# A two-layer encoder on one core: both MLPs begin with two of seven products for eight slab pairs, with the results and the weight sums in DRAM

## The chip, the cores and the metric

The kernel runs on one NeuronCore of one Trainium2 chip. The time is device microseconds of one execution. It was 1729.74 us before, the median of three runs (1729.57 to 1729.74).

## The reference

A trunk of two encoder layers runs over two request groups with shared weights. Each group has 16 meta tokens in front, so there are 272 + 528 = 800 tokens of width 1024. The mixer of layer 0 is latent attention (16 heads); that of layer 1 is grouped-query attention in a window of 128, with sinks. A squared-ReLU MLP follows in both.

```python
def sqrelu_mlp(x, w1, w2):          # 1024 -> 4096 -> 1024
    h = jax.nn.relu(x @ w1)
    return (h * h) @ w2

for i in range(DEPTH):              # DEPTH = 2
    mix = mla_mixer(...) if i % 2 == 0 else gqa_mixer(...)
    h = layer_norm(DN_ALPHA * h + mix, ln1_g[i], ln1_b[i])
    h = layer_norm(DN_ALPHA * h + sqrelu_mlp(h, mlp_w1[i], mlp_w2[i]), ln2_g[i], ln2_b[i])
return h[:, N_META:]
```

All inputs and outputs are float32.

## The kernel before

**Numbers.** A product of float32 matrices is made of three matmuls (`mm3`, lines 547 to 549). Each operand is split into a rounded part and what is left: ScalarE casts the high part (line 1558 for weights, 1601 for activations) and VectorE subtracts (1564, 1603). The tiles `wsp` and `wspi` hold split weights, `h` and `h2` split activations, `w` and `wa` are banks of PSUM.

**Strassen's products.** The 800 tokens lie as columns in two halves of 400 (384 in layer 1, whose meta tokens are dropped). W1's 4096 columns are 32 slabs of 128. A pair of slabs with a pair of halves is a product of 2 x 2 blocks, done with seven products of blocks in place of eight (Winograd's form). It needs sums of weight blocks (`weight_add`, line 1575), sums of activations (`right_operands`, lines 1703 and 1691) and sums of results (`plus`, line 1785; `minus`, line 1609). `up_pair` does this for a pair; `down_group` does W2 likewise for two pairs at a time and adds into `acc` (lines 1869 and 1871). One pair's seven products have 12 matmuls each.

**The start of an MLP.** When an MLP begins, half 0 of the tokens is normed and half 1 is not. Its LayerNorm (`layer_norm`) is a chain: a matmul that gives the mean (line 1644), eight subtractions, squares, and sums of squares (1646, 1652, 1654), a matmul with ones (1661), root and reciprocal, a matmul that spreads the scale (1670), eight multiplications (1675). The sum over channels, `ssum` and `sqsum`, has been added up on GpSimd (line 1384) while the out-projection of the attention wrote `acc`. TensorE meanwhile has four slabs, `UP_FIRST`, done the plain way (eight products of eight): `up_slab` for half 0, and later for half 1, then `down_first` with four rows of W2. The other 28 slabs follow in six groups of two pairs and a last one (`LAST`).

```python
for j in UP_FIRST:
    F[j, 0] = split_hidden(up_slab(j, 0, ws[j], twos, fill.get(j)))
for k in range(4):
    right_operands(k)
for j in range(UPN):
    F[j, 1] = split_hidden(up_slab(j, 1, w, ...))
down_first()
for g, js in enumerate(GROUPS):
    down_group(g, [{} for _ in js], js)
```

**What sets the order.** `Plan` collects tasks with an engine, a cost, and what each reads and writes. It then writes out one order for every engine. TensorE's order comes from a table (`ORDERS`); the others' order, and for some sums the engine (`either`: VectorE or GpSimd), come from the planner's costs. Each engine works through its list in order, and so does the queue of SyncE (SP), which has all loads and stores of the MLPs. Weights pass through four raw tiles (`wraw`) and four split tiles; `sq` tiles hold results on the way.

Of the kernel before, what the change touches and what calls it, by code (L numbers as in the profile page):

```python
# [2756 lines left out]
```

## Time and profile before

| | |
|---|---|
| median of three runs | 1729.74 us |
| profiled execution | 1731.45 us, of which span 1729.7 us |
| granted TensorE clock | 0.998 |
| busy: TensorE, VectorE, ScalarE, GpSimd | 1715.9, 1427.1, 1022.0, 273.8 us |
| MLP 0, MLP 1 | about 449 to 917, 1231 to 1690 us |

A timeline row has the start, the busy time, engine, line, operation, what it writes and reads, shape and count, and in brackets the idle time of the engine before it and what ended that. In rows of groups the bar parts the names from busy time, mean ns of one, and idle time. In windows each engine has its busy time in the stretch, with the number of instructions; then come TensorE's granted clock, the busy share of the DMA engines and what they moved. A row of DMA issues has the KB of one transfer and the microseconds from issue to landing.

### The profile page before, as it was taken

To read this page: it belongs to the slowest core of one execution; us is meant where nothing else is said; L and a number is where in the kernel's file an instruction comes from. 1 tells how busy PE (TensorE), PEld (TensorE's weight loads), DVE (VectorE), ACT (ScalarE), POOL (GpSimd) and SP (SyncE) were. 2 spreads that over 40 slices of the span, in tenths; PEclk is the share of its full clock that TensorE was granted. 3 is DMA by queue.
4 is the path that set the end of the run, shared out by engine and by line. 5 is a ranking of instruction groups with operands and counts; after the bars stand their busy time and mean duration, and the time that the engine had idled before them with its cause. 6 is when DMAs were issued, how large, how long until landed. Compare 5 with 4: busy or idle time off the path is not lost.

```text
span 1729.7 us, 28705 instructions
## 1 busy us (share of the span) xinstructions
PE 1715.9 (99%) x10826; PEld 1619.1 (94%) x10826; DVE 1427.1 (83%) x2916; ACT 1022.0 (59%) x2176; POOL 273.8 (16%) x311
## 2 busy tenths in 40 slices
PE   9999999999999999999999999999999999999998
PEld 8999999989999999999999998889989889988996
DVE  7788878776878889899886978876887898899977
ACT  6577777773746446545644728775655446554652
POOL 1243222322200000000002233232200000000000
PEclk9999999999999999999999999999999999999999
DMA  6111100105211221222112321112211221221122
GB/s 232 59 41 32 32 26 26 40 30 170 95 57 54 74 74 62 74 74 74 62 67 99 102 90 53 38 38 83 101 55 56 74 72 64 73 86 61 62 81 90
DMA packets 39019, 122.32 MB, mean 71 GB/s; under 512 B 4704, under 2 KB 9952, under 8 KB 38752
## 3 DMA queue, kind: packets, MB, share of 16 engines
q1 hardware_dynamic: 38448, 120.09, 20.4%
q8 instruction: 85, 1.39, 0.3%
q14 instruction: 54, 0.44, 0.1%
q10 hardware_dynamic: 432, 0.39, 0.1%
HBM read 117.32 MB, written 3.15 MB: 70 GB/s over the span
## 4 chain that ended last, share of the span: by engine, by line
PE 96%; DVE 3%; ACT 1%; DMA 0%; issue 0%; SPq 0%; DVEq 0%; ACTq 0%
PE w L548 18%; PE w L547 18%; PE w L549 18%; PE wb L547 4%; PE wb L548 4%; PE wb L549 4%; PE wa L547 3%; PE wa L549 3%; PE wa L548 3%; PE wa L1291 2%; PE wa L1258 2%; PE sa L547 2%; PE sa L548 2%; PE sa L549 2%; PE wb L2459 2%; PE wb L2441 1%
## 5 line engine op out<-in xcount | busy, mean ns | idle before, releaser
L1871 DVE TENSOR_TENSOR acc<-acc,w 128x400 f32<-128x400 f32 (+1 forms) x306 | 184.8, 620 | 32.7 <-PE w L549 30.9
L548 PE MATMUL w<-h,wspi 128*128 128x400 f32 x320 | 110.3, 345 | 0.0
L547 PE MATMUL w<-h,wspi 128*128 128x400 f32 x320 | 110.1, 344 | 0.0
L549 PE MATMUL w<-h,wspi 128*128 128x400 f32 x320 | 110.1, 344 | 0.0
L548 PE MATMUL w<-h,wsp 128*128 128x400 f32 x312 | 107.7, 345 | 0.0
L547 PE MATMUL w<-h,wsp 128*128 128x400 f32 x312 | 107.6, 345 | 0.0
L549 PE MATMUL w<-h,wsp 128*128 128x400 f32 x312 | 107.4, 344 | 0.0
L1603 DVE TENSOR_TENSOR h<-sq,h 128x384 fp32r<-128x384 f32 (+1 forms) x163 | 91.2, 571 | 10.6 <-ACT h L1601 10.0
L1601 ACT CAST h<-sq 128x384 fp32r<-128x384 f32 (+1 forms) x163 | 82.8, 519 | 23.7 <-DVE sq L1609 13.8
L1200 ACT ACTIVATE p<-sa,nm,rq 106x528 f32<-106x528 f32 (+1 forms) x80 | 63.4, 794 | 24.4 <-DVE nm L1197 22.4
L547 PE MATMUL w<-wsp,h 128*128 128x512 f32 (+1 forms) x178 | 69.6, 391 | 0.8 <-DVE acc L1871 0.8
L549 PE MATMUL w<-wsp,h 128*128 128x512 f32 (+1 forms) x178 | 69.4, 390 | 0.0
L548 PE MATMUL w<-wsp,h 128*128 128x512 f32 (+1 forms) x178 | 69.4, 390 | 0.0
L547 PE MATMUL w<-wspi,h 128*128 128x512 f32 x174 | 69.0, 396 | 0.0
L549 PE MATMUL w<-wspi,h 128*128 128x512 f32 x174 | 68.8, 395 | 0.0
L548 PE MATMUL w<-wspi,h 128*128 128x512 f32 x174 | 68.8, 395 | 0.0
L1196 DVE TENSOR_REDUCE nm<-sa 106x1 f32<-106x528 f32 (+1 forms) x80 | 55.7, 701 | 14.8 <-PE sa L549 14.2
L547 PE MATMUL sa<-k,q 128*106 128x264 f32 (+5 forms) x208 | 62.7, 301 | 1.6 <-ACT p L1200 1.4
L1782 ACT COPY sq<-w 128x400 f32<-128x400 f32 (+1 forms) x71 | 34.5, 486 | 49.2 <-PE w L549 48.5
L1227 POOL TENSOR_TENSOR p<-p,rs 106x512 f32<-106x512 f32 (+1 forms) x40 | 42.0, 1049 | 129.6 <-DVE pk L1218 93.3
L547 PEld LDWEIGHTS w<-h,wspi 128*128 128x128 f32 x320 | 60.1, 188 | 0.0
L548 PEld LDWEIGHTS w<-h,wspi 128*128 128x128 f32 x320 | 60.1, 188 | 0.1
(847 smaller groups left out, 6086.8 us busy)
## 6 DMA issues: line engine op xcount, KB each, us to landing
wrawo<-in_w_o_dram SPq DMA_DIRECT2D x32, 512.0 KB, 3.3
wraw0d<-in_w2b_dram SPq DMA_DIRECT2D x24, 512.0 KB, 3.3
wraw1d<-in_w2b_dram SPq DMA_DIRECT2D x18, 512.0 KB, 3.3
wrawq<-in_w_q_dram SPq DMA_DIRECT2D x8, 512.0 KB, 3.3
xr<-in_xT_dram SPq DMA_DIRECT2D x16, 200.0 KB, 3.4
wraw<-in_w_qn_dram SPq DMA_DIRECT2D x8, 384.0 KB, 3.0
wx1d<-in_w2b_dram SPq DMA_DIRECT2D x6, 512.0 KB, 4.4
out_dram<-fo SPq DMA_DIRECT2D x11, 256.0 KB, 2.1
```

The costliest lines, as they stand in the source:

```text
L547: first = nc.tensor.matmul(out, lh, rh, start=start, stop=False, **kw)
L548: nc.tensor.matmul(out, lh, rl, start=False, stop=False, **kw)
L549: last = nc.tensor.matmul(out, ll, rh, start=False, stop=stop, **kw)
L1196: plan.task("DVE", DVE(528), lambda: V.tensor_reduce(nm.t[:qm, 0:1], v(), axis=AX.XY, op=ALU.max, negate=True), reads=[ps], writes=[nm], n ...
L1200: lambda: S.activation(P_().rearrange("p (a b) -> p a b", b=264), v(), AF.Exp, bias=nm.t[:qm, 0:1], scale=sc, accum_out=rs.t[:qm, 0:1]),
L1227: f = lambda row=row, r=r, w=w: G.tensor_tensor(row()[:, META:T], row()[:, META:T], r().to_broadcast([qm, w]), ALU.mult)
L1258: nc.tensor.transpose(ps.t[:, k * qm : (k + 1) * qm], src[k], ident[:qm, :qm])
L1291: nc.tensor.matmul(av[64 * e : 64 * e + 64, :n], vt.t[:, k, h0 + 64 * e : h0 + 64 * e + 64], PT.t[:, e, k, :n], start=k == 0, stop=False, ...
L1601: plan.task("ACT", 530, lambda: S.copy(d.t[:, 0], c.t[:, :n]), reads=[c], writes=[(d, "hi")], new=[d])
L1603: "DVE", 570, lambda: V.tensor_tensor(d.t[:, 1], c.t[:, :n], d.t.bitcast(F32)[:, 0], ALU.subtract),
L1871: f = lambda: V.tensor_tensor(z, z, ps.t[:, : z.shape[-1]], ALU.add)
L2459: nc.tensor.matmul(av[64 * gi : 64 * gi + 64, :256], at["V"][:, kbs[k][0], gc : gc + 64], PT.t[:, a : a + 256], start=k == 0, stop=False, ...
```

## The change

`UP_FIRST` becomes the eight even slabs from 0 to 14, which stand for eight pairs, and every pair goes by seven products. The signs of the Winograd form change, so that two of the seven products use only half 0 (`B1`), one with a plain block of W1 each. `head_pair` does these two for all eight pairs while half 1 is normed; the results leave through ScalarE (the second also through ReLU and square) and are stored to DRAM (`keep`, line 1808). In the groups `cross` does one more product, with a sum of weights that is loaded for two pairs at a time, and `rest_pair` does the other four; both fetch the kept results (`fetch`, line 1811). The three parts of the LayerNorm are put in after 1, 8 and 10 half products (`hooks`).

The eight pairs' weight sums, and those of W2 for two groups (`PRESUMS`), are made in DRAM: `presum` puts 24 transfers of 1 MB a layer into GpSimd's queue, each row of 2048 floats; 12 copy and 12 add to what is there. Layer 0's run during attention 0, layer 1's early in MLP 0. `halves` loads the sums as two blocks of 256 KB. The slab loop's `up_slab` and `down_first` go, and there are seven groups. For the pairs left, `weight_add` gives way to `sum_on`, in one instruction for 1024 columns where there were two of 512. The number of `sq` tiles goes from 6 to 8, all four tables of TensorE's order are new, and the planner has one more resource, `SUM`, with 10 us for a transfer.

```diff
-UP_FIRST = (3, 0, 1, 2)
-UPN = len(UP_FIRST)
+UP_FIRST = (tuple(range(0, 16, 2)), tuple(range(0, 16, 2)))
+SQ = (8, 8)
 LAST = 28
-GROUPS = [(j, j + 2) for j in range(UPN, LAST, 4)]
+PRESUMS = 2
+SUM_TIME = 10000
+GROUPS = [(j, j + 2) for j in range(0, LAST, 4)]
...
 ORDERS = [
-    "0 3 2 4-5 8 6 9 7 1 12-13 11 10 16 14 17 15 20 19 18 23 21-22 29 24 26-28 30 32 31 25 33 35 37-40 36 34 41 46 42 45 44 47-49 51 "
+    "0 3 2 4-5 8 6 9 7 1 12-13 11 10 16 14 17 15 20 19 18 23 21-22 29 24 26-28 30 32 31 25 33 35 37-38 34 36 39-41 46 42 45 44 47-49 51"
...
+    presums = [
+        {"up": spill.tile([4, len(UP_FIRST[l]), P, 512], F32, tag=f"us{l}", name=f"us{l}"), "down": spill.tile([4, PRESUMS, P, 1024], F32, tag=f"ds{l}", name=f"ds{l}")}
...
+    def presum(plan, l, last):
...
+                    op = {"accum_op": ALU.add} if key in seen else {}
...
+                    f = lambda x=x, a=a, op=op, out=out, c=c: nc.gpsimd.dma_start(out[x, c], a, **op, **size)
+                    plan.task("POOL", 1500, f, reads=[*reads, *last], writes=[on])
+                    plan.task("SUM", SUM_TIME, lambda: None, reads=[on], writes=[key, ("sum", l)])
+                    last = [("sum", l)]
...
-            split_weights(ua, lo, a, lo)
-            weight_add((a, lo), (a, lo), (b, lo), ALU.subtract, 512)
-            weight_add((b, lo), (b, lo), (b, hi), ALU.add, 512)
+            sum_on((a, lo), (b, lo))
+            sum_on((b, lo), (b, hi))
...
+        def keep(i, x, c):
+            plan.task("SP", 2600, lambda: nc.sync.dma_start(kept[i, x], c.t[:, :n]), reads=[c], writes=[("kept", i, x)])
+
+        def fetch(i, x, c):
+            plan.task("SP", 2600, lambda: nc.sync.dma_start(c.t[:, :n], kept[i, x]), reads=[("kept", i, x)], writes=[c], new=[c])
+            return c
...
+        def head_pair(i, w, ps):
...
+                    yield product(ps, w, lo, B1, 0, True, False, True, ks)
+                    if ks[-1] == 3:
+                        copy(a, ps)
+                        keep(i, 0, a)
...
+                    yield product(ps, w, hi, B1, 4, False, True, False, ks)
+                    if ks[-1] == 3:
+                        copy(c, ps, AF.Relu, 1.0)
+                        square_slow(c)
+                        keep(i, 1, c)
...
+        def rest_pair(i, D):
...
+            ua = halves(f"{j}x", summed(0, i), summed(1, i))
+            a, r = fetch(i, 0, tmp(f"a{l}_{j}r")), tmp(f"r{l}_{j}")
+            product(X, ua, lo, Ts[0], 0, True, False, True)
...
+            D[1] = split_hidden(fetch(i, 1, tmp(f"c{l}_{j}s")))
+            product(X, ua, hi, Ts[1], 0, False, False, False)
...
+            ub = halves(f"{j}y", summed(2, i), (w1[j + 1][:, hi], []))
+            product(X, ub, lo, Ts[2], 0, False, False, False)
...
+            c = fetch(i, 1, tmp(f"c{l}_{j}r"))
...
+            product(X, ub, hi, B2, 0, False, True, False)
...
+        hooks = {1: mean, 8: sums, 10: scale}
+        if l == 0:
+            presum(plan, 1, [(("h", 1, 7), "lo")])
```

**VectorE at the LayerNorm of MLP 0, before.** `acc` is the half being normed, `w_1` the mean's bank, `sq_0` and `sq_1` the two running sums of squares, `wspi` a split weight.

```order
L1646 TENSOR_TENSOR acc<-acc,w_1_5637 128x400 x4
L1564 TENSOR_TENSOR wspi_687<-wraw0f_5633,wspi_687 128x1024
L1646 TENSOR_TENSOR acc<-acc,w_1_5637 128x400 x2
L1652 TENSOR_TENSOR sq_1_5671<-sq_1_5671,sq_3_5682 128x400
L1646 TENSOR_TENSOR acc<-acc,w_1_5637 128x400 x2
L1652 TENSOR_TENSOR sq_0_5657<-sq_0_5657,sqsum_5240 128x400
L1652 TENSOR_TENSOR sq_0_5657<-sq_0_5657,sq_3_5682 128x400
L1652 TENSOR_TENSOR sq_1_5671<-sq_1_5671,sq_4_5697 128x400
L1654 TENSOR_TENSOR sq_0_5657<-sq_0_5657,sq_1_5671 128x400
L1564 TENSOR_TENSOR wspi_724<-wraw0f_5640,wspi_724 128x1024
L1665 RECIPROCAL rst_5623<-rst_5623 100x4
```

**The same, after.**

```order
L1674 TENSOR_TENSOR acc<-acc,w_1_5682 128x400 x6
L1680 TENSOR_TENSOR sq_1_5704<-sq_1_5704,sq_3_5718 128x400
L1674 TENSOR_TENSOR acc<-acc,w_1_5682 128x400 x2
L1680 TENSOR_TENSOR sq_0_5694<-sq_0_5694,sq_5_5725 128x400
L1680 TENSOR_TENSOR sq_0_5694<-sq_0_5694,sqsum_5253 128x400
L1680 TENSOR_TENSOR sq_1_5704<-sq_1_5704,sq_2_5707 128x400
L1682 TENSOR_TENSOR sq_0_5694<-sq_0_5694,sq_1_5704 128x400
L1589 TENSOR_TENSOR wspi_689<-wraw0f_5679,wspi_689 128x1024
L1589 TENSOR_TENSOR wspi_726<-wraw0f_5684,wspi_726 128x1024
L1693 RECIPROCAL rst_5653<-rst_5653 100x4
```

The split of a weight that stood between the subtractions now stands behind the chain's last sum.

**GpSimd at the end of attention 0, before.** `p` is a softmax tile, `ssum` and `sqsum` the sums over channels of the first and the second half.

```order
L1227 TENSOR_TENSOR p_4997<-p_4997,rs_4998 104x512
L1384 TENSOR_TENSOR ssum_4697<-acc 128x400
L1384 TENSOR_TENSOR ssum_4697<-ssum_4697,acc 128x400 x4
L911 TENSOR_TENSOR sqa_5323<-sqa_5323,sqa_5335 128x400
L911 TENSOR_TENSOR sqa_5332<-sqa_5332,sqa_5348 128x400
L1384 TENSOR_TENSOR sqsum_5240<-acc 128x400
L1384 TENSOR_TENSOR sqsum_5240<-sqsum_5240,acc 128x400 x4
L1703 TENSOR_TENSOR tsum_5635<-acc 128x400
L1652 TENSOR_TENSOR sq_0_5657<-sq_0_5657,sq_2_5674 128x400
```

**The same, after.** `ds` is the DRAM tile with the sums of W2, `in_w2q` the weights in the order in which they are added.

```order
L1251 TENSOR_TENSOR p_5009<-p_5009,rs_5010 104x512
L967 DMA ds_869<-in_w2q_dram 128x2048 x2
L1408 TENSOR_TENSOR ssum_4710<-acc 128x400
L1408 TENSOR_TENSOR ssum_4710<-ssum_4710,acc 128x400 x2
L967 DMA ds_869<-ds_869 128x2048
L1408 TENSOR_TENSOR ssum_4710<-ssum_4710,acc 128x400 x2
L967 DMA ds_869<-in_w2q_dram 128x2048
L911 TENSOR_TENSOR sqa_5350<-sqa_5350,sqa_5363 128x400
L911 TENSOR_TENSOR sqa_5360<-sqa_5360,sqa_5375 128x400
L1408 TENSOR_TENSOR sqsum_5253<-acc 128x400
L967 DMA ds_869<-ds_869 128x2048
L1408 TENSOR_TENSOR sqsum_5253<-sqsum_5253,acc 128x400
```

Transfers now stand between the additions to `ssum` and `sqsum`; one with `ds` on both sides reads what an earlier one made.

**SP's queue early in MLP 0, before.** All rows are loads of W1 and W2.

```order
L1533 DMA wraw0a_5769<-in_w2a_dram 128x1024
L1533 DMA wraw_4a<-in_w_0_dram 128x1024
L1533 DMA wraw_4b<-in_w_0_dram 128x1024
L1533 DMA wraw_6a<-in_w_0_dram 128x1024
L1533 DMA wraw_6b<-in_w_0_dram 128x1024
L1533 DMA wraw0d_6221<-in_w2b_dram 128x1024
```

**The same, after.** `us` is the DRAM tile with the sums of W1.

```order
L1558 DMA wraw0f_5729<-in_w_0_dram 128x1024
L1808 DMA kept_5654<-sq_6_5727 128x400
L1808 DMA kept_5656<-sq_3_5718 128x400
L1558 DMA wraw0f_5771<-in_w_0_dram 128x1024
L1558 DMA wraw0f_5791<-in_w_0_dram 128x1024
L1808 DMA kept_5658<-sq_5_5725 128x400
L1839 DMA wraw_x_5821<-us_868 128x512 x2
L1808 DMA kept_5655<-sq_4_5722 128x400
L1808 DMA kept_5660<-sqsum_5253 128x400
L1839 DMA wraw_0x<-us_868 128x512 x2
L1839 DMA wraw_2x<-us_868 128x512 x2
L1839 DMA wraw_0y<-us_868 128x512
```

Stores of kept results now stand between the loads of slabs and of weight halves.

More of the change, by code (lines that the diff above doesn't have):

```diff
@@ L148 @@
 class Plan:
-    LAG = {"PE": 198, "DVE": 45, "ACT": 45, "POOL": 50, "SP": 0}
+    LAG = {"PE": 198, "DVE": 45, "ACT": 45, "POOL": 50, "SP": 0, "SUM": 0}
     CHANGE = {
@@ L157 @@
     }
-    OVER = {"PE": 0, "DVE": 82, "ACT": 100, "POOL": 30, "SP": 0}
+    OVER = {"PE": 0, "DVE": 82, "ACT": 100, "POOL": 30, "SP": 0, "SUM": 0}
     last, count = {}, 0
@@ L477, in tile_encoder @@
     wp = pool("wp")
+    spill = pool("spill", space=bass.MemoryType.DRAM)
     banks = {}
@@ L1476, in attention0 @@
                     after0[o, i]()
-        ahead = [t.weights(ins["w1_0"][j], f"up{j}") for j in UP_FIRST[:2]]
+        ahead = [t.weights(ins["w1_0"][j], f"up{j}") for j in UP_FIRST[0][:2]]
         for x in ahead:
@@ L1482, in attention0 @@
             plan.issue(after)
-        for j, x in zip(UP_FIRST, ahead):
+        for j, x in zip(UP_FIRST[0], ahead):
             W.give(("up", j), x.t)
@@ L1569, in wparts, with sum_on @@
             return [h, *[(p, x) for p in parts(h, c) for x in ("hi", "lo")]]
[L1571 to L1576 removed]
+        def sum_on(out, x):
+            (r, c), key = out, parts(*out)
+            either(c.stop - c.start, lambda e: e.tensor_tensor(r.t[:, c], r.t[:, c], x[0].t[:, x[1]], ALU.add), reads=[*key, *parts(*x)], writes=key)
         lo, hi = slice(0, 512), slice(512, 1024)
@@ L1758, in residual, with up_tools, product @@
             return transposes
-        def up_pair(j, operands, beside=None, over=()):
-            ua, ub, uc, w22 = up_weights(j)
-            B = [([x[:, hf] for x in h], "h", hf) for hf in range(2)]
-            Ts = [([x[:, i] for x in T], "T", i) for i in range(3)]
-            def product(ps, w, c, X, k0, start, stop, fresh):
+        B1, B2 = [([x[:, hf] for x in h], "h", hf) for hf in range(2)]
+        Ts = [([x[:, i] for x in T], "T", i) for i in range(3)]
+        def up_tools(over=()):
+            def product(ps, w, c, X, k0, start, stop, fresh, ks=range(4)):
                 x = X[0]
                 def run():
-                    for k in range(4):
+                    for k in ks:
                         a = c.start + k * P
@@ L1776, in run @@
                         )
-                reads = [*wparts(w, c), *acts(X[1], X[2], range(k0, k0 + 4))]
-                plan.task("PE", 12 * MM, run, reads=reads, writes=[ps], new=[ps] if fresh else [], ends=over)
-            def copy(d, ps, f=AF.Copy):
-                plan.task("ACT", 500, (lambda: S.copy(d.t[:, :n], ps.t[:, :n])) if f is AF.Copy else (lambda: S.activation(d.t[:, :n], ps.t[:, :n], f)), reads=[ps], writes=[d], new=[d])
+                reads = [*wparts(w, c), *acts(X[1], X[2], [k0 + k for k in ks])]
@@ L1784, in plus, with copy @@
+                plan.task("PE", 3 * len(ks) * MM, run, reads=reads, writes=[ps], new=[ps] if fresh and ks[0] == 0 else [], ends=over)
+            def copy(d, ps, f=AF.Copy, scale=-1.0):
+                plan.task(
+                    "ACT", 500, (lambda: S.copy(d.t[:, :n], ps.t[:, :n])) if f is AF.Copy else (lambda: S.activation(d.t[:, :n], ps.t[:, :n], f, scale=scale)),
+                    reads=[ps], writes=[d], new=[d],
+                )
             def plus(d, ps):
                 plan.task("DVE", 570, lambda: V.tensor_tensor(d.t[:, :n], d.t[:, :n], ps.t[:, :n], ALU.add), reads=[ps, d], writes=[d])
-            def square(d, relu=True):
-                if d in (a, r, b, e):
-                    if relu:
-                        plan.task("ACT", 510, lambda: S.activation(d.t[:, :n], d.t[:, :n], AF.Relu), reads=[d], writes=[d])
-                    plan.task("ACT", 510, lambda: S.activation(d.t[:, :n], d.t[:, :n], AF.Square), reads=[d], writes=[d])
-                    return
-                plan.task(
-                    "DVE", 575, lambda: V.scalar_tensor_tensor(d.t[:, :n], d.t[:, :n], 0.0, d.t[:, :n], ALU.max, ALU.mult),
-                    reads=[d], writes=[d], port=True,
-                )
@@ new lines, in square @@
+            def square(d, scale=1.0):
+                if scale:
+                    plan.task("ACT", 510, lambda: S.activation(d.t[:, :n], d.t[:, :n], AF.Relu, scale=scale), reads=[d], writes=[d])
+                square_slow(d)
+            return product, copy, plus, square
+        def keep(i, x, c):
[3 more added lines that the diff above has]
+            return c
@@ new lines, in head_pair, with first, second @@
+        def head_pair(i, w, ps):
+            product, copy, plus, square = up_tools()
+            a, c = tmp(f"a{l}_{i}"), tmp(f"c{l}_{i}")
+            def first():
+                for ks in (range(0, 2), range(2, 4)):
+                    yield product(ps, w, lo, B1, 0, True, False, True, ks)
+                    if ks[-1] == 3:
+                        copy(a, ps)
+                        keep(i, 0, a)
+            def second():
+                for ks in (range(0, 2), range(2, 4)):
+                    yield product(ps, w, hi, B1, 4, False, True, False, ks)
[3 more added lines that the diff above has]
+                        keep(i, 1, c)
+            return first, second
@@ new lines, in halves, with summed @@
+        def halves(nm, *srcs):
+            r, w = new("wraw", lambda: wp.tile([P, 1024], F32, tag="wraw", name=f"wraw{l}_{nm}", bufs=WRAW)), weights(f"{l}_{nm}")
+            for x, (c, (src, key)) in enumerate(zip((lo, hi), srcs)):
+                plan.task("SP", 1900, lambda r=r, c=c, src=src: nc.sync.dma_start(r.t[:, c], src), reads=key, writes=parts(r, c), new=[r] if x == 0 else [])
+            for c in (lo, hi):
+                split_weights(w, c, r, c)
+            return w
+        def summed(x, i):
+            return presums[l]["up"][x, i], []
@@ L1798, in up_pair @@
+        def up_pair(j, operands, beside=None, over=()):
+            ua, ub, uc, w22 = up_weights(j)
+            product, copy, plus, square = up_tools(over)
             X, Y, Z = bank(f"ux{l}_{j}"), bank(f"uy{l}_{j}"), bank(f"uz{l}_{j}")
@@ L1807, in up_pair @@
                     tiles[j + o] = [None, None]
-            product(X, ua, lo, B[1], 0, True, False, True)
-            copy(a, X)
+                product(Z, uc, hi, B1, 4, True, True, True)
+                plus(a, Z)
+                square(a)
+                plain(0, 0, a)
+                product(X, ub, lo, Ts[1], 0, False, False, False)
+                copy(b, X)
+                product(X, uc, lo, Ts[2], 0, False, False, False)
+                copy(e, X)
+                product(X, w22, lo, B2, 0, False, True, False)
+                copy(r, X, AF.Relu)
+                square(r, False)
+                plain(1, 0, r)
+                product(Y, ua, hi, Ts[0], 0, True, False, True)
+                plus(e, Y)
+                square(e, -1.0)
+                plain(1, 1, e)
+                if beside is not None:
+                    beside()
+                product(Y, ub, hi, B2, 4, False, True, False)
+                plus(b, Y)
+                square(b)
+                plain(0, 1, b)
+                return
             product(Y, ua, hi, Ts[0], 0, True, False, True)
@@ L1856, in down_weights @@
-            weight_add((A11, c), (A21, c), (A11, c), ALU.add, w)
-            split_weights(out[5], c, A11, c)
-            A12 = raw(src[3, :, :w], f"{l}d{g}3", "wx" if l else "wraw")
-            weight_add((A21, c), (A12, c), (A21, c), ALU.subtract, w)
-            split_weights(out[3], c, A21, c)
-            split_weights(out[4], c, A22, c)
-            split_weights(out[2], c, A12, c)
+            get = lambda x, tag="wraw": raw(src[x, :, :w], f"{l}d{g}{x}", tag)
+            if g < PRESUMS:
+                out = {}
+                for x in DOWN_ORDERS[l]:
+                    i = {1: 0, 4: 2, 2: 3}.get(x)
+                    r = raw(presums[l]["down"][{5: 0, 7: 1, 6: 2, 3: 3}[x], g], f"{l}d{g}s{x}") if i is None else get(i)
+                    out[x] = weights(f"{l}d{g}_{x}")
+                    split_weights(out[x], c, r, c)
+                return out
@@ L1863, in down_weights, with accumulate @@
+            split_weights(out[3], c, A11, c)
+            for x in DOWN_ORDERS[l][5:]:
+                split_weights(out[x], c, A22 if x == 4 else A12, c)
             return out
         seen = set()
-        def accumulate(z, ps, place):
+        def accumulate(z, ps, place, op=ALU.add):
             if l == 0 and place not in seen:
-                f = lambda: V.scalar_tensor_tensor(z, z, ALPHA, ps.t[:, : z.shape[-1]], ALU.mult, ALU.add)
+                f = lambda: V.scalar_tensor_tensor(z, z, ALPHA, ps.t[:, : z.shape[-1]], ALU.mult, op)
@@ L1987, in mlp_middle @@
-        mean, sums, scale = layer_norm()
-        twos = [range(k, k + 2) for k in range(0, 8, 2)]
-        fill = {UP_FIRST[0]: {0: mean}, UP_FIRST[1]: {3: sums}, UP_FIRST[2]: {1: scale}}
-        F = {}
-        for j in UP_FIRST:
-            if j not in ws:
-                ws[j] = up_weight(j)
-            F[j, 0] = split_hidden(up_slab(j, 0, ws[j], twos, fill.get(j)))
+        mean, sums, scale = layer_norm()
+        kept = {(i, x): spill.tile([P, n], F32, tag=f"kept{l}{i}{x}", name=f"kept{l}{i}{x}") for i in range(len(UP_FIRST[l])) for x in range(2)}
@@ new lines, in mlp_middle @@
+        late = {}
+        hooks = {1: mean, 8: sums, 10: scale}
+        if l == 0:
+            presum(plan, 1, [(("h", 1, 7), "lo")])
+        made_ = 0
+        for p in range(0, len(UP_FIRST[l]), 2):
+            two = []
+            for i in (p, p + 1):
+                w = ws[UP_FIRST[l][i]] if UP_FIRST[l][i] in ws else up_weight(UP_FIRST[l][i])
+                two.append(head_pair(i, w, bank(f"ux{l}h{i}")))
+            for x in range(2):
+                for f in two:
+                    for _ in f[x]():
+                        made_ += 1
+                        if made_ in hooks:
+                            hooks[made_]()
@@ L1995, in mlp_middle, with crosses @@
+        turn = residual() if l else None
+        def crosses(i):
+            w = halves(f"x{i}", summed(3, i), summed(3, i + 1))
+            cross(i, w)
+            cross(i + 1, w)
+        crosses(0)
         for k in range(4):
             right_operands(k)
-        turn = residual() if l else None
-        for j in range(UPN):
-            w = up_weight(j) if j == UP_FIRST[0] else ws[j]
-            F[j, 1] = split_hidden(up_slab(j, 1, w, [range(k, k + 1) for k in range(8)] if j == 0 else [range(8)]))
@@ L2001, in mlp_middle @@
-        down_first()
-        for g, js in enumerate(GROUPS):
+        for g, js in enumerate(GROUPS):
+            if g == 0 and turn:
+                for hf, q in TURNS:
+                    turn(hf, q)
+            if js[0] in UP_FIRST[l] and js[0] // 2 not in late:
+                crosses(js[0] // 2)
             down_group(g, [{} for _ in js], js)
@@ L2603, in attention1 @@
                     after1[o, i]()
-        ahead = [weights(ins["w1_1"][j], f"up{j}") for j in UP_FIRST[:2]]
+        ahead = [weights(ins["w1_1"][j], f"up{j}") for j in UP_FIRST[1][:2]]
         for w in ahead:
@@ L2609, in attention1 @@
             plan.issue(after)
-        for j, w in zip(UP_FIRST, ahead):
+        for j, w in zip(UP_FIRST[0], ahead):
             W.give(("up", j), w.t)
```

270 lines of the change are left out of this document (127 added, 143 removed), and 73 rows, old and new, of the table ORDERS.

## The prediction

> **What bounds the kernel now.** I read the engines' busy shares first, then the chain that ended last, then windows by stage, and inside the stages single rows.
>
> ```profile
> span 1729.7 us, 28705 instructions
> PE 1715.9 (99%) x10826; PEld 1619.1 (94%) x10826; DVE 1427.1 (83%) x2916; ACT 1022.0 (59%) x2176; POOL 273.8 (16%) x311
> PE 96%; DVE 3%; ACT 1%; DMA 0%; issue 0%; SPq 0%; DVEq 0%; ACTq 0%
> ...
> core 0: us, PE busy (x) PEld busy (x) DVE busy (x) ACT busy (x) POOL busy (x), PEclk, DMA share, GB/s
> 380.00:449.10 69.10, 69.10 (x417) 66.78 (x416) 48.79 (x69) 32.96 (x55) 19.45 (x13) 1.00 0.43 141
> 449.10:480.00 30.90, 30.73 (x174) 29.88 (x173) 27.07 (x48) 24.61 (x48) 4.40 (x4) 1.00 0.16 55
> 500.00:900.00 400.00, 400.00 (x2196) 399.70 (x2195) 345.23 (x580) 205.42 (x359) 10.95 (x9) 1.00 0.19 66
> 1225.00:1260.00 35.00, 34.10 (x199) 32.27 (x198) 30.05 (x49) 24.91 (x54) 8.24 (x7) 1.00 0.29 95
> 1490.00:1540.00 50.00, 49.24 (x244) 43.73 (x243) 46.32 (x69) 26.87 (x48) 5.59 (x4) 1.00 0.20 64
> ```
>
> TensorE is idle for 13.8 us of 1729.7 and 96% of the chain is its own matmuls. In 500 to 900, inside MLP 0, it is never idle, at full clock. So a matmul less is worth its issue interval, as long as nothing else comes to hold TensorE. The next engine is VectorE: 345.23 of 400 us (86%). Where VectorE is fullest in MLP 1 (46.32 of 50 us, 93%), TensorE loses 0.76 us: that row is my measure of what a crowded VectorE costs. The second weak place is the LayerNorm ahead of each MLP, where everything behind the norm waits for a short serial chain.
>
> **Matmuls removed.** Products 1 and 2 of the eight pairs need only the half that is already normed, so they take the place of the plain slabs as cover, and four slabs a layer go from eight products in eight to seven. Counted in the two instruction orders, TensorE issues 48 matmuls of 400 columns, 24 of 384 and 18 of 512 fewer. The listed means overlap in the pipeline; the price is the distance between starts.
>
> ```profile
> 1250.82 0.34 PE L547 MATMUL w<-hc,wspi 128*128 128x384 f32 x1
> ...
> 1252.90 0.34 PE L547 MATMUL w<-hc,wspi 128*128 128x384 f32 x1
> ...
> 1344.90 0.40 PE L547 MATMUL w<-wsp,h 128*128 128x512 f32 x1
> ...
> 1347.00 0.40 PE L547 MATMUL w<-wsp,h 128*128 128x512 f32 x1
> ```
>
> 400 columns: 400.00/2196 = 0.182 us. 384: 12 starts in 2.08 us, 0.173. 512: 9 starts in 2.10 us, 0.233. So 48 x 0.182 + 24 x 0.173 + 18 x 0.233 = 8.7 + 4.2 + 4.2 = **17.1 us** off the path.
>
> **The LayerNorm's cover.** The norm's chain on VectorE, in both layers:
>
> ```profile
> 450.58 0.94 PE L1644 MATMUL w<-sqsum,part 128*128 128x400 f32 x2 [0.17 <-DVE sqsum L1384]
> ...
> 453.67 1.23 DVE L1564 TENSOR_TENSOR wspi<-wraw0f,wspi 128x1024 fp32r<-128x1024 f32 x1
> ...
> 459.18 0.58 DVE L1654 TENSOR_TENSOR sq<-sq,sq 128x400 f32<-128x400 f32 x1
> ...
> 460.08 0.79 PE L1661 MATMUL w<-ones,sq 128*100 128x1 f32 x8
> ...
> 1230.75 0.94 PE L1644 MATMUL w<-sqsum,part 128*128 128x400 f32 x2 [0.23 <-DVE sqsum L2499]
> 1239.99 0.87 PE L1661 MATMUL w<-ones,sq 128*100 128x1 f32 x8
> ```
>
> Before, 48 matmuls stand between the mean and the sums, which is 8.8 us, and the chain needs 459.76 - 450.58 = 9.2 us with a weight split of 1.23 us in its midst: they fit (0.17 us idle in 449 to 480). Now 36 stand there in layer 0 (6.6 us) and 42 in layer 1 (7.3 us), and the split has left the middle of the chain, which then needs about 9.2 - 1.2 = 8.0 us. With 0.4 us of the mean's own second piece the cover is 7.0 and 7.7, so TensorE would wait about 1.0 us in layer 0 and 0.3 in layer 1. Between the sums and the scale 12 matmuls stand instead of 6, so that wait can't grow. I take +1.3 us; bounds 0 (VectorE's other work in the chain goes too) and 2.2 + 1.5 = 3.7 (the chain stays at 9.2).
>
> **VectorE.** By the orders it issues 130 adds of 512 columns fewer, 52 operations of 1024 more, 47 more of 400 and 22 more of 384 columns.
>
> ```profile
> L1575 DVE TENSOR_TENSOR wraw0d<-wraw0d,wraw0d 128x512 f32<-128x512 f32 x46 | 30.9, 686 | 0.5 <-DMA wraw0d<-in_w2b_dram 0.5
> ...
> L1564 DVE TENSOR_TENSOR wspi<-wraw0d,wspi 128x1024 fp32r<-128x1024 f32 x21 | 25.6, 1221 | 1.6 <-ACT wspi L1558 1.6
> ...
> L1603 DVE TENSOR_TENSOR h<-sq,h 128x384 fp32r<-128x384 f32 x83 | 46.1, 572 | 3.8 <-ACT h L1601 3.6
> L1603 DVE TENSOR_TENSOR h<-sq,h 128x400 fp32r<-128x400 f32 x80 | 45.1, 571 | 6.8 <-ACT h L1601 6.4
> ```
>
> -130 x 0.686 + 52 x 1.221 + 69 x 0.571 = -89.2 + 63.5 + 39.4 = +13.7 us of work, in some 17 us less time. Over the 800 us that VectorE works in the two MLPs that is 814 in about 910, 89%: between the 86% that cost TensorE nothing and the 93% that cost 0.76 us in 50 (1.5%). The four groups a layer of kept pairs take 8 x 288 x 0.182 = 420 us; at 1.5% that is 6.4 us, at the 86% row nothing. I take +1.5, nearer the 86% row, because in the crowded stretch VectorE was also slowed by sums on GpSimd, and ends 0 and 6.4. ScalarE gains 48 operations and loses 40, and is 51% busy in 500 to 900: nothing, covered by matmuls.
>
> **DRAM sums.** 24 transfers a layer of 1 MB, from DRAM to DRAM, 12 copies and 12 that add. GpSimd issues them and waits in its queue for the one that a sum adds to. They lie beside other work; the price is zero if each lands in time. The nearest landings are loads and the final stores:
>
> ```profile
> wrawo<-in_w_o_dram SPq DMA_DIRECT2D x32, 512.0 KB, 3.3
> ...
> out_dram<-fo SPq DMA_DIRECT2D x11, 256.0 KB, 2.1
> ...
> wraw<-in_w_in_dram SPq DMA_DIRECT2D x3, 512.0 KB, 5.9
> ```
>
> From 2.1 and 3.3 us the slope is 1.2 us per 256 KB, so 1 MB takes 0.9 + 4.8 = 5.7 us and an adding one, with two reads, 0.9 + 9.6 = 10.5; in proportion to 512 KB, 6.6 and 13.2. The last row is the start of the kernel, where all loads are under way at once; in proportion to it an adding one would take 23.6. All are estimates: no row shows a DRAM-to-DRAM sum, and the middle ones are nearest: in 380 to 449 the engines are 0.43 busy at 141 GB/s, and the last eight sums, 4 x 1 + 4 x 2 = 12 MB in the 78 us up to 432, add 154 GB/s, by that row 0.47: nearly full, not over. The place that can't bear lateness is the end of attention 0. There the last sums stand between GpSimd's softmax multiplies and the additions whose result the mean waits for:
>
> ```profile
> 364.95 1.04 POOL L1227 TENSOR_TENSOR p<-p,rs 106x512 f32<-106x512 f32 x1 [3.69 <-DVE pk L1218]
> ...
> 407.36 2.17 POOL L1384 TENSOR_TENSOR ssum<-ssum,acc 128x400 f32<-128x400 f32 x2 [11.70 <-DVE acc L1377]
> ...
> 422.06 1.98 POOL L1384 TENSOR_TENSOR sqsum<-acc 128x400 f32<-128x400 f32 x1 [2.04 <-DVE acc L1377]
> 430.53 1.05 POOL L1384 TENSOR_TENSOR sqsum<-sqsum,acc 128x400 f32<-128x400 f32 x1 [6.50 <-DVE acc L1377]
> 436.91 3.26 POOL L1384 TENSOR_TENSOR sqsum<-sqsum,acc 128x400 f32<-128x400 f32 x2 [5.32 <-DVE acc L1377]
> 444.58 1.25 POOL L1384 TENSOR_TENSOR sqsum<-sqsum,acc 128x400 f32<-128x400 f32 x1 [4.42 <-DVE acc L1377]
> ```
>
> In the new order the 18th sum follows the multiply at about 365, and 20, 21, 22, 23 and 24 each wait for the one before, so the last issues no earlier than 366 + 5T (365 and its multiply), T being one transfer. It has its place at about 432: T may be 13.2 us for nothing. Behind it stand three additions, some 5 us, due shortly before the mean's matmul at 450.6, 449.9 with VectorE's last addition. With T from 5.7 to 13.2 I cost it at 0.
>
> **Loads and kept results.** SP issues 170 transfers more, 96 of them the kept results (32 stores, 64 fetches); most of the others are weight halves. A store stands in SP's queue until its result is squared, and the loads behind it wait. The DMA share is 0.19 in MLP 0 at 66 GB/s; layer 1's sums, which run there, move 12 x 1 + 12 x 2 = 36 MB, 77 GB/s over its 468 us, which by that row is 0.22 more: far from full. I cost this at nothing: cover is one weight product, 12 x 0.182 = 2.2 us, against a fetch of about 2 us issued a group earlier. If the cover is gone, a pair loses about 1 us (rival A).
>
> **The sum**, against the profiled execution (1731.45 us, 1.7 over the median of the runs): 1731.45 - 17.1 + 1.3 + 1.5 = 1717.15, and as a median 1717.15 - 1.7 = **1715.4 us**.
>
> **Rivals.**
>
> A. *The gain is eaten by VectorE and late loads.* A kept pair's five products take 60 matmuls, 10.9 us, for five weight halves, their splits and four kept results; before, 84 matmuls covered a pair's weights. For it: 1490 to 1540 above. Against it: 500 to 900, with no idle at 86%. Price: 6.4 us for VectorE and up to 1 us for each of 16 pairs, 22.4 in full. Half of it or all, added to the 1711 that the saving gives without any cost (below): 1722 to 1733.
>
> B, the other side. *The DRAM sums are slow and hold GpSimd's queue ahead of the LayerNorm's sum.* The mean matmul stands in TensorE's queue, so all stops. At T = 16 the last sum issues at 446, and about 1 us is lost; the gain is gone where 366 + 5T + 5 = 449.9 + 14.3, at T = 18.6 us; at the 23.6 us of the start's loads the loss is 39 us, which gives 1715 + 39 = 1754. Against it: the loads of 3.3 us. For it: the DMA engines then are nearly full, each adding transfer waits for the one before to have landed, so delays add five times, and the upper end lies beyond the point that decides. The Trainium skill, DMA: Bandwidth & Descriptors (Two DMAs through the same engine are not ordered), has the dependent transfer wait for the earlier one's semaphore, and its section Anatomy of one DMA says that this can come after a surprisingly long delay when the target is DRAM, although its figure for a transfer from GpSimd's queue (2.0 us plus bytes over 436e3) gives an estimate of 4.4 us for 1 MB. By the figure the sum stays at 1715.4, by the warning it would be B's 1754; no run of before has such a transfer.
>
> C. *The kept results change nothing*, because the LayerNorm's wait grows by what the matmuls save: it would need 7 to 8 us at each norm, three times the worst case above (2.2). About 1727 to 1731.
>
> **How the numbers follow.** Forecast (1709 to 1722) 0.69, A 0.15, B 0.12, C 0.04. Bounds of the forecast: all costs at zero and the 1.7 us idle in the two MLP 1 windows regained gives 1711, with 2 us left for what the trace can't resolve; upwards all ends in full, 3.7 and 6.4 us instead of 2.8, give 1723, where A begins. The range of 8 in 10 reaches into A: 1709 to 1729. A difference of 0.2%, 3.5 us, is about what can be told from no change: below 1726.3 lie the forecast and half of A, 0.77; within, 0.10, the other half of A with C; above 1733.2, 0.13, B and a remnant of A.
>
> **What would show it.** Right: some 90 matmul records fewer; TensorE without gaps in 500 to 880; sums landing in under 13 us; the mean's row 0.2 us after its sum; VectorE near 89% in the MLPs. Wrong: an idle time of several us ahead of the mean matmul put down to GpSimd's sum (B), gaps at first products of kept pairs put down to weight splits or fetches (A), over 2 us before the matmul with ones in either layer (C).

## The result, and the profile after

The changed kernel takes 1741.88 us (median of four runs, 1740.68 to 1743.99) against 1729.74: a ratio of 1.0069, interval 1.0051 to 1.0086. It is slower by 12 us, where 14 us less were forecast, and it lies outside the range of 1709 to 1729. The profiled execution took 1743.99 us.

The page of the profile after, its first lines, the DMA queues and the first rows of the DMA issues (KB of one, and us to landing):

```profile
span 1742.2 us, 29013 instructions
...
PE 1708.4 (98%) x10736; PEld 1609.0 (92%) x10736; DVE 1431.2 (82%) x2911; ACT 1027.0 (59%) x2184; POOL 299.2 (17%) x353
...
q1 hardware_dynamic: 62928, 157.20, 27.0%
q0 software_dynamic: 6912, 50.33, 11.2%
...
PE 89%; DVE 5%; DMA 4%; ACT 2%; issue 1%; SPq 0%; DVEq 0%; ACTq 0%
...
us<-in_w1q_dram POOLq DMA_DIRECT2D x24, 1024.0 KB, 8.7
...
ds<-in_w2q_dram POOLq DMA_DIRECT2D x12, 1024.0 KB, 8.2
```

TensorE's records are 90 fewer, as the orders say. But it is idle for 33.8 us instead of 13.8, and the chain that ended last now holds 4% of DMA, where before it held none. The times of the mean's matmul in the two layers divide the loss:

```profile
450.74 0.94 PE L1672 MATMUL w<-sqsum,part 128*128 128x400 f32 x2 [0.17 <-DVE sqsum L1408]
...
1254.54 0.94 PE L1672 MATMUL w<-sqsum,part 128*128 128x400 f32 x2 [0.23 <-DVE sqsum L2580]
```

Up to MLP 0 nothing has changed (450.58 before). From one mean to the other it is 803.8 us instead of 780.2: 23.6 more. From the second mean to the end it is 487.7 instead of 498.9: 11.3 less. So the same form of MLP wins in layer 1 and loses in layer 0. Windows over MLP 0, over a stretch in it, over MLP 1, and the end of attention 0 (columns as before: us, busy time of the engines, clock, DMA share, GB/s):

```profile
545.00:580.00 35.00, 22.47 (x91) 20.85 (x92) 15.82 (x28) 7.40 (x15) 2.75 (x4) 0.77 1.01 295
449.10:917.00 467.90, 447.42 (x2397) 441.69 (x2396) 393.60 (x653) 240.41 (x426) 25.57 (x32) 0.97 0.51 155
1231.00:1690.00 459.00, 458.60 (x2356) 416.90 (x2355) 409.91 (x639) 264.31 (x482) 36.54 (x31) 1.00 0.35 114
...
380.00:449.10 69.10, 69.10 (x418) 66.58 (x417) 48.00 (x73) 33.26 (x55) 20.00 (x19) 1.00 0.82 238
```

In MLP 0 TensorE is idle for 20.5 us; in 545 to 580 it does 91 matmuls in 35 us, and the DMA engines have no free time at all. What it waits for in MLP 0, the chain through that stretch, and GpSimd's timeline:

```profile
PE w L547 <- ACT sq L1793: 11.2, 5, 6.9
PE w L547 <- ACT wspi L1583: 7.1, 2, 5.1
...
461.08 16.19 DMA wraw0f<-in_w_dram
...
551.66 22.79 DMA wraw_6y<-in_w_dram
```

```profile
456.52 2.45 POOL L967 DMA_DIRECT2D us<-in_w1q_dram  x4
534.22 1.05 POOL L1636 TENSOR_TENSOR sq<-sq,sq 128x400 f32<-128x400 f32 x1 [75.25 <-DVE h L1626]
535.22 2.51 POOL L967 DMA_DIRECT2D us<-in_w1q_dram  x3
536.82 1.44 POOL L967 DMA_DIRECT2D us<-us  x1
544.27 0.55 POOL L967 DMA_DIRECT2D us<-us  x1 [6.01 <-DMA us<-in_w1q_dram]
```

The waits name ScalarE's splits and copies, but ScalarE was waiting itself: a load of 512 KB issued at 461.1 landed after 16.2 us, one of 256 KB issued at 551.7 after 22.8, where before loads of 512 KB took 3.3. Ahead of each, GpSimd had put four of layer 1's sums into its queue within some 3 us (at 456.5, and at 535.2 with a fifth at 544.3). In attention 0, softmax multiplies or other work stood between nearly all sums; in MLP 0, from 456 to 580, GpSimd's own work between them is one square. Layer 1's sums are not over early in MLP 0, either: the last are issued at 778. In 449 to 600 the sums themselves land after some 12 and 13 us, half as long again as on the whole:

```profile
us<-in_w1q_dram POOLq DMA_DIRECT2D x9, 1024.0 KB, 11.9
us<-us POOLq DMA_DIRECT2D x4, 1024.0 KB, 13.4
```

The stops cost more than themselves. TensorE's timeline behind two of them:

```profile
560.75 0.70 PE L547 MATMUL w<-t,wspi 128*128 128x400 f32 x1 [5.13 <-ACT wspi L1583]
...
575.54 0.70 PE L547 MATMUL w<-t,wspi 128*128 128x400 f32 x1 [6.89 <-ACT sq L1793]
576.04 0.54 PE L548 MATMUL w<-t,wspi 128*128 128x400 f32 x1
...
580.38 0.54 PE L549 MATMUL w<-t,wspi 128*128 128x400 f32 x1
580.71 0.44 PE L547 MATMUL w<-t,wspi 128*128 128x400 f32 x1
```

For 5.2 us after the second stop matmuls start 0.334 us apart instead of 0.182. Windows over four such stretches, behind stops of 2.0, 5.1, 6.9 and 2.0 us, have a granted clock of 0.50 to 0.62:

```profile
474.20:478.70 4.50, 3.83 (x12) 3.48 (x13) 2.95 (x5) 2.39 (x4) 0.00 (x0) 0.62 1.01 357
560.70:567.40 6.70, 6.41 (x18) 5.83 (x19) 4.88 (x10) 1.14 (x3) 0.82 (x1) 0.51 0.99 272
575.50:580.90 5.40, 5.36 (x16) 5.32 (x17) 3.00 (x5) 2.92 (x4) 0.54 (x1) 0.50 1.00 394
683.20:686.80 3.60, 3.60 (x12) 3.60 (x13) 2.25 (x5) 0.22 (x1) 0.00 (x0) 0.53 0.61 196
```

Their 58 matmuls take 19.2 us, some 9 more than at 0.182 each. Over all of MLP 0, TensorE's busy time is 447.4 - 2397 x 0.182 = some 11 us above that pace. With the 20.5 idle that is some 32, as much as the 23.6 lost and the 8.7 that the missing matmuls save come to.

### The profile page after: what moved, and what is told of

Its sections match the earlier page's. It is cut to its first block, busy times and chain, and to the rows that moved or that the text cites. A ratio compares the mean times of both kernels' runs of the same rounds, so it can differ in the third digit from the quotient of the medians.

```text
span 1742.2 us, 29013 instructions
## 1 busy us (share of the span) xinstructions
PE 1708.4 (98%) x10736; PEld 1609.0 (92%) x10736; DVE 1431.2 (82%) x2911; ACT 1027.0 (59%) x2184; POOL 299.2 (17%) x353
## 4 chain that ended last, share of the span: by engine, by line
PE 89%; DVE 5%; DMA 4%; ACT 2%; issue 1%; SPq 0%; DVEq 0%; ACTq 0%
PE w L547 16%; PE w L548 16%; PE w L549 16%; PE wb L547 4%; PE wb L548 4%; PE wb L549 4%; PE wa L547 3%; PE wa L549 3%; PE wa L548 3%; PE wa L1315 2%; PE wa L1282 2%; PE sa L547 2%; PE sa L549 2%; PE sa L548 2%; PE wb L2540 2%; PE wb L2522 1%
## 5 line engine op out<-in xcount | busy, mean ns | idle before, releaser
L1626 ACT CAST h<-sq 128x400 fp32r<-128x400 f32 (+1 forms) x161 | 82.0, 518 | 59.9 <-DMA sq<-kept 30.9
L1626 DVE TENSOR_TENSOR h<-sq,h 128x400 fp32r<-128x400 f32 (+1 forms) x161 | 91.7, 581 | 21.8 <-ACT h L1626 21.3
L547 PE MATMUL w<-h,wspi 128*128 128x400 f32 x292 | 101.2, 346 | 2.0 <-ACT wspi L1583 1.9
L549 PE MATMUL w<-h,wspi 128*128 128x400 f32 x292 | 101.1, 346 | 0.6 <-DVE wspi L1589 0.6
L548 PE MATMUL w<-h,wspi 128*128 128x400 f32 x292 | 100.9, 345 | 0.0
L1636 POOL TENSOR_TENSOR sq<-sq,sq 128x384 f32<-128x384 f32 (+1 forms) x20 | 23.0, 1151 | 367.7 <-DVE h L1626 189.2
L1798 DVE TENSOR_TENSOR sq<-sq,w 128x384 f32<-128x384 f32 (+1 forms) x101 | 56.6, 560 | 30.9 <-PE w L549 27.3
L1224 ACT ACTIVATE p<-sa,nm,rq 106x528 f32<-106x528 f32 (+1 forms) x80 | 63.3, 793 | 21.6 <-DVE nm L1221 17.9
L547 PE MATMUL w<-t,wspi 128*128 128x400 f32 (+1 forms) x180 | 63.4, 352 | 12.0 <-ACT sq L1793 6.9
L547 PE MATMUL w<-t,wsp 128*128 128x384 f32 (+1 forms) x204 | 70.8, 347 | 3.1 <-ACT sq L1793 2.0
L547 PE MATMUL w<-wspi,h 128*128 128x512 f32 (+1 forms) x182 | 71.6, 393 | 0.0
L549 PE MATMUL w<-wspi,h 128*128 128x512 f32 (+1 forms) x182 | 71.6, 393 | 0.0
L548 PE MATMUL w<-wspi,h 128*128 128x512 f32 (+1 forms) x182 | 71.5, 393 | 0.0
L548 PE MATMUL w<-t,wsp 128*128 128x384 f32 (+1 forms) x204 | 70.6, 346 | 0.0
L549 PE MATMUL w<-t,wsp 128*128 128x384 f32 (+1 forms) x204 | 70.4, 345 | 0.1
L1802 ACT ACTIVATE sq<-sq 128x384 f32<-128x384 f32 (+1 forms) x86 | 45.5, 529 | 34.9 <-DVE sq L1798 34.5
L547 PEld LDWEIGHTS w<-h,wsp 128*128 128x128 f32 x324 | 61.2, 189 | 3.7 <-ACT sq L1793 3.3
```

Of the source, the lines that this page charges most:

```text
L547: first = nc.tensor.matmul(out, lh, rh, start=start, stop=False, **kw)
L548: nc.tensor.matmul(out, lh, rl, start=False, stop=False, **kw)
L549: last = nc.tensor.matmul(out, ll, rh, start=False, stop=stop, **kw)
L1224: lambda: S.activation(P_().rearrange("p (a b) -> p a b", b=264), v(), AF.Exp, bias=nm.t[:qm, 0:1], scale=sc, accum_out=rs.t[:qm, 0:1]),
L1626: return lambda: S.copy(hi(), view()), lambda: V.tensor_tensor(lo(), view(), hi().bitcast(F32), ALU.subtract)
L1798: plan.task("DVE", 570, lambda: V.tensor_tensor(d.t[:, :n], d.t[:, :n], ps.t[:, :n], ALU.add), reads=[ps, d], writes=[d])
```

## Experiments

Theory T1: layer 1's sums, several at once early in MLP 0, crowd out its loads. Rival T2, from the prediction's A: loads and fetches of kept pairs are late by themselves. All runs but `e9_paced_small` start from the changed kernel, and all were timed with the kernel before on the same chip (1729.89 to 1731.69 us there).

**Layer 1's sums elsewhere.** `e1_att1_sums`:

```diff
-        if l == 0:
-            presum(plan, 1, [(("h", 1, 7), "lo")])
 ...
+        presum(plan, 1, [("ex", *ITEMS[0])])      # in attention1
```

> Layer 1's 24 DRAM sums are issued in attention 1, between GpSimd's softmax multiplies, instead of early in MLP 0; all else as in the changed kernel. Theory T1 (these sums, four and more under way at once, crowd out MLP 0's loads and fetches, which then land after 16 to 23 us): TensorE's idle time in MLP 0 falls from 20 us to under 3, the clock there returns to 1.00, and the time falls to 1711 to 1717 us. Rival T2 (loads and fetches of kept pairs are late by themselves, for SP's queue and four raw tiles): idle stays at 15 us or more in MLP 0, time 1736 to 1743.

Measured: 1758.65 us, ratio 1.0157 (1.0142 to 1.0172). Both forecasts missed the time; the trace decides. (Here and in `e7_att1_early` the prompt group's numbers are others; TensorE does the same 10736 matmuls.) Its window over MLP 0, TensorE's longest wait, and GpSimd's rows at the second LayerNorm:

```profile
449.10:917.00 467.90, 466.14 (x2558) 464.07 (x2556) 409.42 (x679) 260.65 (x463) 12.47 (x11) 1.00 0.35 111
...
PE w L1689 <- DVE sq L1682: 30.9, 1, 30.9
...
1252.93 0.54 POOL L967 DMA_DIRECT2D ds<-ds  x1 [10.64 <-DMA ds<-in_w2q_dram]
1258.37 0.80 POOL L967 DMA_DIRECT2D ds<-in_w2q_dram  x1 [4.89 <-DMA ds<-ds]
1266.27 0.53 POOL L967 DMA_DIRECT2D ds<-ds  x1 [7.10 <-DMA ds<-in_w2q_dram]
1271.69 0.81 POOL L967 DMA_DIRECT2D ds<-in_w2q_dram  x1 [4.90 <-DMA ds<-ds]
1272.24 2.28 POOL L1680 TENSOR_TENSOR sq<-sq,sq 128x400 f32<-128x400 f32 x2
```

MLP 0 has lost its idle time (1.8 us), against T2. The time went to the other end: the last sums, each waiting for the one before, now stand in GpSimd's queue ahead of two additions of the LayerNorm, and TensorE stands for 30.9 us. That is rival B's mechanism, at another place than B had it. It is not the whole loss: from one mean's matmul to the other the run takes 783.4 us (453.91 to 1237.27), some 10 more than `e2_no_sums_l1` below (449.25 to 1222.86), so the sums cost time in attention 1 as well.

**The sums left out.** `e2_no_sums_l1` and `e3_no_sums`:

```diff
-            return presums[l]["up"][x, i], []
+            return (ins["w1q_1"] if l else presums[l]["up"])[x, i], []   # e3: ins[f"w1q_{l}"][x, i]
 ...                                                                     # W2's sums likewise
-        if l == 0:
-            presum(plan, 1, [(("h", 1, 7), "lo")])                      # e3: and layer 0's presum
```

> Layer 1's DRAM sums are left out: its groups load plain weight blocks of the same size where the sums would be, so layer 1's products are of other numbers. T1: MLP 0 as in the run with the sums in attention 1, time within 2 us of it (1710 to 1716); what it is below that run is the price of the sums in attention 1. T2: 1736 to 1743.

> The DRAM sums of both layers are left out, plain blocks loaded in their place (other numbers). Its distance to the run without layer 1's sums is the price of layer 0's sums in attention 0. T1: 0 to 2 us, since the trace shows TensorE full in 150 to 450 with them. T2 says nothing on it but that MLP 0 stays at 15 us idle.

Measured: 1715.96 us (1712.34 to 1716.45), ratio 0.9907 (0.9892 to 0.9922); and 1712.06 (1711.92 to 1712.23), ratio 0.9889 (0.9872 to 0.9905). The windows over MLP 0 and MLP 1 of the run without any sums:

```profile
449.10:917.00 467.90, 466.18 (x2558) 464.44 (x2558) 409.21 (x679) 263.61 (x467) 12.48 (x11) 1.00 0.34 110
1231.00:1690.00 459.00, 458.82 (x2334) 414.03 (x2332) 405.70 (x638) 261.94 (x477) 28.32 (x24) 1.00 0.34 111
```

T1 holds, T2 falls: with kept results, fetches and weight halves, but no sums, TensorE is idle for 1.7 us in MLP 0 and 0.2 in MLP 1. Layer 1's sums cost some 26 us (1741.88 - 1715.96; by the ratios, 1.0069 and 0.9907, 28), layer 0's 0 to 4, where 0 to 2 were forecast (the ranges of the two runs nearly touch).

**Behind the kept pairs.** `e4_sums_behind`:

```diff
+            if l == 0 and g == 3:
+                plan.task("POOL", 200, lambda: G.tensor_copy(gate, acc[:, 0, 0, :1]), reads=[("acc", 0, 0)], writes=["gate"])
+                presum(plan, 1, ["gate"])
```

> Layer 1's sums are held by a one-column copy on GpSimd until the fourth group of MLP 0 has added to acc, so they run beside the three groups without kept pairs, up to eight at once. T1 in its general form (any loads are crowded out): the idle time moves from 450 to 580 to some 720 to 800, 5 to 20 us of it, time 1718 to 1735. T1 if only the small loads and fetches of kept pairs are that tender: under 3 us idle, 1711 to 1717. T2: idle stays in 450 to 580, 1736 to 1743.

Measured: 1733.57 us, ratio 1.0016 (1.0007 to 1.0025). Windows ahead of the first sum and behind it:

```profile
449.10:690.00 240.90, 239.66 (x1318) 237.92 (x1317) 215.04 (x364) 139.79 (x249) 7.58 (x7) 1.00 0.45 144
690.00:917.00 227.00, 215.09 (x1146) 210.28 (x1145) 182.94 (x300) 106.83 (x191) 19.59 (x27) 0.98 0.61 175
```

The idle time has moved with the sums, 11.9 us of it, to groups that fetch nothing kept. So T1 holds in its general form: loads of other groups are hit as well.

**Paced, or in smaller pieces.** What hurts could be how many sums are under way (T1a), how much is moved (T1b), or the size of their pieces (T1c). `e5_paced` puts a copy of one column, which waits for a given addition to `acc`, ahead of each sum; `e6_small_packets` halves the pieces; `e7_att1_early` has the sums in attention 1 from its start.

```diff
+            if held and len(adds) % 8 == 4:                                  # e5, in accumulate
+                plan.task("POOL", 200, lambda: G.tensor_copy(gate, z[:, :1]), reads=[place], writes=["gate"])
+                held.pop(0)("gate")
-        size = {"max_dma_last_dim": 8192}
+        size = {"max_dma_last_dim": 4096 if l else 8192}                     # e6
+        presum(plan, 1, [])                                                  # e7, in attention1, none in MLP 0
```

> Layer 1's sums stay in MLP 0 but are paced: ahead of each one GpSimd copies one column of acc that a given product has just been added to, every eighth addition, so one sum is issued some 18 us after the other, over all seven groups. Theory T1a (what hurts is several transfers of 1 MB under way at once): idle in MLP 0 under 4 us, 1712 to 1719 us. Rival T1b (what hurts is the amount moved beside MLP 0's loads, however spread): 1725 to 1738.

> As the changed kernel, but layer 1's sums are cut into pieces of half the size (the limit on one piece 4096 instead of 8192); issue times and bytes are the same. Rival T1c (the big pieces of a sum get more than their share of the DMA engines beside the loads' smaller ones): the loads in 450 to 600 land earlier, idle falls by 5 us or more, 1728 to 1736. T1a and T1b: no difference or slower, 1740 to 1746.

> Layer 1's sums in attention 1 from its start, between GpSimd's multiplies, without waiting for the first softmax, so they are over before the LayerNorm's sums on GpSimd come (in the run e1_att1_sums the last six were still in GpSimd's queue there and held the chain by 30.9 us). T1a: no idle in MLP 0, none at the LayerNorm: 1711 to 1717 us. If the transfers also crowd out attention 1's loads: 1718 to 1728.

Measured: paced 1714.32 us, ratio 0.9907 (0.9891 to 0.9924); smaller pieces 1719.04, 0.9930 (0.9915 to 0.9945); early in attention 1 1719.83, 0.9938 (0.9923 to 0.9952). The windows of the last over part of attention 1, and of the paced run over the bad stretch and MLP 0:

```profile
1000.00:1100.00 100.00, 95.51 (x732) 87.31 (x732) 78.18 (x266) 59.26 (x180) 35.69 (x49) 0.98 0.45 131
```

```profile
545.00:580.00 35.00, 35.00 (x194) 35.00 (x194) 30.27 (x52) 19.48 (x33) 2.25 (x4) 1.00 0.61 194
449.10:917.00 467.90, 465.79 (x2549) 461.71 (x2549) 409.47 (x679) 263.12 (x467) 43.90 (x59) 1.00 0.54 164
```

The same bytes in the same MLP cost about 2 us once they are spread, so T1b falls. In attention 1 TensorE is idle for 4.5 us at the softmax. The time lies in the range that was given for the case that the sums also crowd out attention 1's loads; but what TensorE waits for there is VectorE's softmax, and whether late loads stand behind that was not followed up. Smaller pieces gained 23 us, against T1a's forecast and more than T1c's. But their trace shows a second thing, the fourth sum held back until the second had landed (at 466.7), though nothing stood between in the queue:

```profile
457.14 1.69 POOL L967 DMA_DIRECT2D us<-in_w1q_dram  x3
467.03 0.92 POOL L967 DMA_DIRECT2D us<-in_w1q_dram  x1 [8.20 <-issue]
```

If more pieces fill GpSimd's ring of descriptors, fewer sums are under way. `e8_short_ring` parts the two, and `e9_paced_small` has the paced sums in small pieces:

```diff
-    nc = bacc.Bacc("TRN2", ..., dynamic_dma_scratch_size=1024)
+    nc = bacc.Bacc("TRN2", ..., dynamic_dma_scratch_size=512)                # e8
```

> As the changed kernel, pieces of the sums as they were (8192), but GpSimd's ring of descriptors has half the length, so that about as few sums can be under way at once as in e6_small_packets, where the smaller pieces filled the ring. T1a (the number under way): the same gain as there, 1716 to 1725 us. T1c (the size of the pieces): no gain, 1738 to 1746.

> The paced kernel with both layers' sums in the smaller pieces. T1a: paced sums are alone already, so the same as e5_paced within 2 us (1712 to 1717). T1c: what is left between that run and the one without any sums (1714.3 and 1712.1) goes: 1712 to 1713.

Measured: 1717.63 us, ratio 0.9926 (0.9911 to 0.9941), pieces unchanged: T1a, and the ring alone gives all that the smaller pieces gave. Paced in small pieces: 1713.94, 0.9900 (0.9883 to 0.9916), no different from paced. GpSimd's row of the short ring shows the same hold as above, and its rows for 545 to 580 follow, with the DMA queues in that stretch (packets, MB, share) and a load, and then the queues and the same load of the changed kernel:

```profile
468.94 0.85 POOL L967 DMA_DIRECT2D us<-in_w1q_dram  x1 [8.39 <-issue]
...
545.00:580.00 35.00, 34.45 (x188) 33.62 (x187) 28.73 (x51) 20.04 (x35) 4.11 (x6) 1.00 1.01 304
...
q0 software_dynamic: 699, 5.07, 56.2%
q1 hardware_dynamic: 2156, 5.53, 44.3%
...
wraw_6y<-in_w_dram SPq DMA_DIRECT2D x1, 256.0 KB, 6.3
```

```profile
q0 software_dynamic: 956, 6.94, 73.5%
q1 hardware_dynamic: 1592, 3.36, 27.8%
...
wraw_6y<-in_w_dram SPq DMA_DIRECT2D x1, 256.0 KB, 22.8
```

The DMA engines are as full in both, 1.01. What differs is who has them. Counted from issue to landing, up to four sums are under way at once there in the changed kernel, 2.4 on the mean, and at most two, 1.6 on the mean, with the short ring. With fewer under way the loads get 44.3% of their time instead of 27.8%, and TensorE loses 0.6 us there instead of 12.5. Why a longer queue of sums gets the larger share, the runs don't tell.

## Where the prediction was right and wrong

- **The matmuls** (17.1 us) were right. Without any sums the gain is 1731.36 - 1712.06 = 19.3 us, near the 18.8 that the prediction's lower bound takes (the matmuls and 1.7 us of idle time regained), and TensorE's busy time falls from 1715.9 to 1697.4.
- **The LayerNorm's cover** (1.3 us) had about the right size, but by luck. The wait it priced, ahead of the matmul with ones, came in neither layer; in layer 0 TensorE waited 0.9 us earlier, for banks that ScalarE had to empty. That matmul follows the mean's by 8.8 us in layer 0 and 8.4 in layer 1, where 8.0 had been worked out for both:

```profile
455.70 0.45 PE L547 MATMUL w<-h,wsp 128*128 128x400 f32 x1 [0.73 <-ACT sq L1793]
...
459.57 0.79 PE L1689 MATMUL w<-ones,sq 128*100 128x1 f32 x8
```

- **VectorE** (1.5 us) cost less than that. Its work grew as forecast, from 800.0 to 814.9 us of the two windows' 926.9 (88%) without sums, and TensorE's idle time there is 1.7 and 0.2 us, of which the 0.9 above is a part. Rival A had this and late loads as its parts. Its sign, gaps at kept pairs put down to weight splits, did show in the changed kernel, but its cause did not hold: without sums the loads cost next to nothing.
- **The DRAM sums**, taken at 0, are the step that failed. The duration was right on the whole, medians of 5.9 to 8.7 us where 5.7 to 13.2 had been worked out, though single sums in the crowded stretch took up to 22.2. At the end of attention 0 they fit: the mean's matmul did not move, and the DMA engines were 0.82 busy where the prediction's row comes to 0.43 + 0.47. But there alone were they looked at one by one. For layer 1's the prediction divided 36 MB by the 468 us of MLP 0 and found 0.22 of the DMA engines, "far from full". The order gave no such spread: nothing in GpSimd's queue holds them, the planner's 10 us for a transfer is no wait on the chip, and in 545 to 580 the share was 1.01. The term measures some 26 us.
- **Loads and kept results**, at 0, were right by themselves (the run without sums), and wrong beside the sums, since a landing of about 2 us had been assumed for a fetch; in 545 to 580 the median of two was 21.6.
- **Rival B** had the mechanism of waiting sums right (30.9 us where they were moved), with the wrong place. Its point of decision, T over 18.6 us at the end of attention 0, was not near: the last four sums there landed after 5.7 to 9.6 us. The Trainium skill, DMA: Bandwidth & Descriptors (Anatomy of one DMA), gives an estimate of 4.4 us for 1 MB from GpSimd's queue by its fit. Most of these took about twice that, and 11.9 to 13.4 in the crowded stretch.
- **Not thought of**: that a stop slows TensorE for some time after it, 5 to 6 us behind the two long ones. The Trainium skill, TensorE: Matmul & The Clock Gate (Part 1), has the clock at half after idle time, until the array has been busy for about 3.4 us. The trace agrees on the half (granted clock 0.50 and 0.51), and here it took 5.2 and 6.5 us.

The paced kernel, at 0.9907, beats the kernel before and the changed one: it keeps the change and takes about 2 us more than the kernel without sums.

## What to carry to other kernels

Read the traffic that a change adds in the stretch where its order puts it, not over its stage: ask what in the issuing queue comes between two transfers, and if nothing does, they all start together. A planner's time for a transfer paces nothing on the chip; a copy of one column that waits for progress, or a shorter ring, does. Work moved to a quieter place brings its queue along, so look at what stands behind it there.

## What had not been expected of the hardware

- With the DMA engines full in both kernels (1.01), the same 256 KB load took 22.8 us with up to four 1 MB sums under way and 6.3 with at most two; the sums' share of the engines' time was 73.5% and 56.2%.
- After stops of 5.1 and 6.9 us matmuls of 400 columns started 0.33 us apart for 6.5 and 5.2 us. Two stops of 2 us were also followed by half the clock. Some 9 us of the loss in MLP 0 is this.
- Halving the pieces of a DRAM sum acted as halving GpSimd's ring did: GpSimd waited 8.2 and 8.4 us to issue the fourth, and the times were 1719.04 and 1717.63 us.
